# A two-layer hybrid decoder (FoX and NSA attention): narrower last values product, two query projections placed earlier, two more fill steps before the compression's products

## The chip, the cores and the metric

The kernel runs on one core of one Trainium2 chip. The metric is the device time of one execution in microseconds (us), as the median of several runs. The profile is that of one more execution; its span goes from the first to the last instruction that the profiler saw.

Names: PE is TensorE's matmul, PEld its weight load, DVE is VectorE, ACT is ScalarE, POOL is GpSimd, SP is SyncE, which issues most DMAs here.

## The reference

A batch of one, 512 tokens, model width 1024, two layers, float32. Each layer:

```
h    = rmsnorm(x);  proj = h @ w_in
y_a  = fox_attention(q_a, k_a, v_a, log_sigmoid(f_a + b)) @ w_o_fox        # 8 heads of 64, causal
kc,vc = compress(kc), compress(vc)     # blocks of 32 keys, stride 16: gelu(flat @ w1 + b1) @ w2 + b2
o_n  = g0 * attn(q_b, kc, vc) + g1 * attn(q_b, ks, vs, selected) + g2 * attn(q_b, kw, vw, window)
y_b  = o_n @ w_o_nsa                                                       # 8 query heads, 2 key heads
x    = x + (sigmoid(gate_a) * y_a + sigmoid(gate_b) * y_b) @ w_out
x    = x + relu(rmsnorm(x) @ w_up)**2 @ w_down                             # width 4096
```

At the end there is a last rmsnorm. With 512 tokens there are 8 selection blocks and up to 16 may be chosen, and the window is 512 wide, so the selected and the window branch are both plain causal attention.

## The kernel before

**Products in float32r halves.** Every large product is split into a high and a low half: the weight into `wh`, `wl`, the activation into `uh`, `ul` (or `oh`, `ol`). A k-tile is then three matmuls of 512 tokens: `wh` by `uh` (L208), `wh` by `ul` (L209), `wl` by `uh` (L210), in `gemm` (L202). A projection with eight k-tiles is 24 matmuls into one PSUM bank of the tag `mm`; its generator yields after every second k-tile, six matmuls. An output `half` (FoX or NSA output projection) has four k-tiles, 12 matmuls. PSUM has four tags of two banks each: `mm` (projections and outputs), `S` (scores), `PT` (transposed probabilities), `O` (attention output, and the compression's first products).

**Weights.** They arrive by SP's DMA in the order that `order` lists (L166), are rounded to `wh` by ACT (L182) and subtracted into `wl` by DVE (L183). Two `raw`, two `wh` and two `wl` buffers alternate. `order` must list the weights in the order in which the products take them.

**Attention.** A head and branch is a unit: 8 units for FoX, 16 for NSA (selected and window for each head) in each layer. `attend` (L464) runs three units staggered: `scores` of one, `transposes` of the one before, `values` of the one before that. Scores go by four query blocks of 128, each two matmuls (L388, L391) as wide as the causal keys (256, 256, 384, 512), a maximum with mask on DVE (L394), an exponent on ACT (L395); after the fourth block come the reciprocal (L399), NSA's gate (L401) and the scaling of the four blocks (L404). Transposes (L417) put 10 blocks of 128 by 128 in three groups into `PT`; ACT copies each group into `pth` (L426), DVE subtracts into `ptl` (L427). Values (L443) multiply them with the values of four key blocks, 512, 384, 256 and 256 wide, once for `pth` and once for `ptl`. The fourth key block needs only the last 128 queries. Its product reads 256 columns, of which the first 128 are a zero block: the third group is laid out as [zeros, (3,3), (2,2), (3,2)], and two memsets on DVE (L424, L425) write the zeros for each unit. The scores of block 0 are computed 256 wide where 128 are used.

**The fill.** Between the steps of attention, `attend` draws steps from a generator `fill`, 1.8 for each attention step in FoX and 0.95 in NSA. In FoX, `fill1` gives the projections of the next heads and the compression of `kc` and `vc`: 16 copies and some small ones from `tmp` into `ca` on DVE (L502, L504, L507), in two steps, and then the first products (L521, plain float32, `ca` as weights), which alternate with the rest of the projections. In NSA, `fill2` gives the softmax over compressed keys (`cmp_gen`, L578 to L620), the gate projections with their `tanh` (L838, L839), the FoX output `half(0, m)` with its multiplication by the gate into `MA` (L848), and the query projections 2 and 3 (`qproj`), whose rotary part takes two `tmp` buffers (L323 to L327) and whose two halves are copied by SP's DMA into `q` (L362). The tag `tmp` has three buffers, which the gate tiles use too.

A tile scheduler fixes the order of each engine's instructions when the kernel is built, so the order in the trace isn't strictly that of the source. Each engine then works off its queue in order.

Of the kernel before, what the change touches and what calls it, by code (L numbers as in the profile page):

```python
# [11 lines left out]
F32 = mybir.dt.float32  # L12
# [128 lines left out]
class Body:  # L141
# [264 lines left out]
    def transposes(self, u):  # L406
        nc = self.nc
        E = u["E"]
        u["pt"] = []
        for g in range(3):  # L410
            ps = self.p("PT")
            if g < 2:
                todo = [(i, g) for i in range(g, NB)]
            else:
                todo = [(3, 3), (2, 2), (3, 2)]
            for j, (i, b) in enumerate(todo):
                nc.tensor.transpose(ps[:, j * 128:(j + 1) * 128], E[i][:, b * 128:(b + 1) * 128], self.ident)  # L417
            n = 128 * len(todo)
            h = self.t("t2", [128, T], F32R, name="pth")
            lo = self.t("t2", [128, T], F32R, name="ptl")  # L420
            o = 0
            if g == 2:
                o = 128
                nc.vector.memset(h[:, :128].bitcast(F32), 0.0)  # L424
                nc.vector.memset(lo[:, :128].bitcast(F32), 0.0)  # L425
            nc.scalar.copy(h[:, o:o + n], ps[:, :n])  # L426
            nc.vector.tensor_sub(lo[:, o:o + n], ps[:, :n], h[:, o:o + n].bitcast(F32))  # L427
            u["pt"].append((h, lo))
            yield

    def values(self, u):
        nc = self.nc
        if u.get("first", True):
            u["O"][0] = self.p("O")
        O = u["O"][0]
        first = u.get("first", True)
        pt = u["pt"]
        last = u.get("last", True)
        todo = [(0, 0, 0, 512), (1, 1, 0, 384), (2, 2, 256, 256), (3, 2, 0, 256)]
        for b, g, o, n in todo:  # L440
            v = u["v"](b)
            for f in range(2):
                nc.tensor.matmul(O[:, T - n:], v, pt[g][f][:, o:o + n],  # L443
                                 start=first and b == 0 and f == 0, stop=last and b == 3 and f == 1)
            yield
        if "after" in u:
            u["after"]()
# [233 lines left out]
    def order(self, l):  # L681

        a = self.a
        flat = lambda ap: ap.rearrange("p k c -> p (k c)")
        wb = [flat(a["wb"][l, i]) for i in range(32)]
        for c in range(4):
            s = a["wva"][l, c]
            if l == 0 and c == 0:
                yield from ((s[:, j], 512) for j in range(2))
            else:  # L690
                yield flat(s), 1024
        yield from ((flat(a["wg2"][l, c]), 576) for c in range(4))
        for i in (0, 1, 2, 3, 8, 9, 4, 5, 6, 7, 10, 12, 13, 11):
            yield wb[i], 1024
        wo = [[flat(a["wo"][l, f, m]) for m in range(4)] for f in range(2)]
        for m in range(8):
            yield wb[16 + m], 1024
            if m % 2 == 1:
                yield wo[0][m // 2], 1024
            if m in (1, 3):  # L700
                yield wb[14 + m // 2], 1024
        yield from ((wb[24 + m], 1024) for m in range(8))
        yield from ((wo[1][m], 1024) for m in range(4))
        yield from ((flat(a["wout"][l, m]), 1024) for m in range(8))
        for c in range(4):
            yield from ((flat(a["wup"][l, 8 * c + j]), 1024) for j in range(8))
            yield from ((flat(a["wdn"][l, c, m]), 1024) for m in range(8))

    def layer(self, l, u):
        nc, a = self.nc, self.a  # L710
        wb = a["wb"][l].rearrange("m p k c -> m p (k c)")
# [5 lines left out]
        g = self.token_proj(src, 512, va, u)  # L717
# [6 lines left out]
        g = self.token_proj([[a["wg2"][l, c].rearrange("p j m -> p (j m)")] for c in range(4)], 288, g2, u)  # L724
# [35 lines left out]
        def proj(i, key, fn, tag="mm"):  # L760
            def done(ps):
                st[key] = fn(ps)
            return self.block(wb[i], u, done, tag)
# [17 lines left out]
        def fox_proj(p, tags=("mm", "mm")):  # L781
            yield from proj(2 * p, ("ka", p), lambda ps: self.k_pair(self.scaled(ps), p), tags[0])
            yield from proj(2 * p + 1, ("qa", p), lambda ps: self.q_pair(self.scaled(ps), True), tags[1])

        def qproj(p):
            return proj(12 + p, ("qb", p), lambda ps: self.q_pair(self.roped(ps)))

        def cmp_gen(hk):
            yield from self.cmp_probs(hk, [st.get(("qb", p)) for p in range(4)])

        def fill1():
            yield from fox_proj(1)
            yield from proj(8, "kc", self.scaled)
            yield from proj(9, "vc", self.scaled)
            c = self.compress(st["kc"], st["vc"], small, l)
            rest = chain(fox_proj(2), fox_proj(3), proj(10, "ks", lambda ps: self.k_pair(self.roped(ps))),
                         qproj(0), qproj(1))
            yield from alternate(c, rest)
            yield from proj(11, "kw", lambda ps: self.k_pair(self.roped(ps)))

        self.pc = {}
        run(fox_proj(0, ("PT", "PT")))
        self.attend([fox_unit(h) for h in range(8)], fill1(), self.FOX_FILL)


# [23 lines left out]
        def half(kind, m, w):  # L829

            xs = ya if kind == 0 else yb
            ps = self.p("mm")
            yield from self.gemm(ps, w, 4 * (m % 2), xs, ks=4)
            st["y"] = ps

        def gate_tanh(ps, tag="tmp"):
            s = self.t(tag, [128, T], name="gate")
            nc.vector.tensor_mul(s, ps, R)  # L838
            nc.scalar.activation(s, s, AF.Tanh, scale=0.5)  # L839
            return s  # L840

        def gated(m0):
            for m in (m0, m0 + 1):
                yield from proj(16 + m, ("ga", m), gate_tanh)
            w = self.weights(a["wo"][l, 0, m0 // 2].rearrange("p i c -> p (i c)"))
            for m in (m0, m0 + 1):
                yield from half(0, m, w)
                nc.vector.scalar_tensor_tensor(MA[m // 2][:, m % 2], st["ga", m], 1.0, st["y"],  # L848
                                               op0=OP.add, op1=OP.mult)

        def fill2():
            yield from cmp_gen(0)
            yield from gated(0)
            yield from qproj(2)
            yield from gated(2)
            yield from qproj(3)
            yield from cmp_gen(1)
            yield from gated(4)
            yield from gated(6)
            for m in range(8):  # L860
                yield from proj(24 + m, ("gb", m), lambda ps: gate_tanh(ps, ("oh", "ol")[m % 2]))

        units = []
        for h in range(0, 8, 2):
            (a0, b0), (a1, b1) = nsa_units(h), nsa_units(h + 1)
            units += [a0, a1, b0, b1]
        self.attend(units, fill2(), self.NSA_FILL)
        yb = [st["ob", p] for p in range(4)]

# [28 lines left out]
        for m in range(8):  # L898
            ps = self.bank()
# [20 lines left out]
        for c in range(4):  # L920
            acts = []
            for j in range(8):
                ps = self.bank()
# [11 lines left out]
            if c < 3 or l + 1 < L:  # L935
# [3 lines left out]
                for m in range(8):  # L939
                    ps = self.bank()  # L940
# [117 lines left out]
def chain(*gens):  # L1058
    for g in gens:
        yield from g  # L1060


def alternate(a, b):

    live = [a, b]
    while live:
        for g in list(live):
            try:
                next(g)
            except StopIteration:  # L1070
                live.remove(g)
            else:
                yield
# [18 lines left out]
```

## Time and profile before

| | |
|---|---|
| median of 3 runs | 1567.62 us (1567.20 to 1568.24) |
| the profiled execution | 1568.84 us, span 1567.1 us |
| granted TensorE clock, mean | 0.997 |
| busy, share of the span | PE 99%, PEld 82%, DVE 57%, ACT 40%, POOL 17% |
| matmul records | 7580 |

A matmul's duration in the trace is from its start to its modelled end, and matmuls are pipelined: the next one starts before the one ahead has ended. What a product costs in a stream is read from start to start. "[0.70 <-DVE ptl L427]" behind a row is the idle time before it and what ended that.

### The profile page before, as it was taken

The numbers are of one execution on the slowest core, as the hardware profiler recorded it, in microseconds if no ns is written. First come the engines' busy times: TensorE is split into PE (matmuls) and PEld (weight loads), VectorE is DVE, ScalarE is ACT, GpSimd is POOL, SyncE is SP. The second block draws the span as 40 slices with busy tenths as digits, with TensorE's granted clock in tenths as the row PEclk, the third lists the DMA queues.
The fourth block names the chain that finished last, engine by engine and source line by source line (L and its number), as shares of the span: only waits on it lengthen the run. The fifth ranks groups of instructions, "written<-read, shape, count | busy, mean of one in ns | idle before, by whom it ended". The sixth has DMA issues, their size and how long they took to land.

```text
span 1567.1 us, 20162 instructions
## 1 busy us (share of the span) xinstructions
PE 1548.7 (99%) x7580; PEld 1280.8 (82%) x7580; DVE 890.0 (57%) x1815; ACT 631.2 (40%) x1145; POOL 260.0 (17%) x210
## 2 busy tenths in 40 slices
PE   9999999999999999999999999999999999999997
PEld 8877788888888888888887687888888888888887
DVE  5687988866443333333646789887564433333343
ACT  6444655643432222223433456555434312222243
POOL 4000000000241322305400000000002504132252
PEclk9999999999999999999999999999999999999998
DMA  6645522133332233223535543222322322332231
GB/s 234 173 130 148 139 69 82 55 100 105 104 94 95 94 97 104 95 94 101 173 118 164 161 124 105 69 67 65 123 96 94 95 94 94 98 104 94 95 121 54
DMA packets 56624, 169.40 MB, mean 108 GB/s; under 512 B 7344, under 2 KB 8112, under 8 KB 56528
## 3 DMA queue, kind: packets, MB, share of 16 engines
q1 hardware_dynamic: 53072, 161.84, 33.3%
q10 hardware_dynamic: 3456, 6.29, 1.2%
q8 instruction: 59, 0.97, 0.3%
q14 instruction: 37, 0.30, 0.1%
HBM read 140.77 MB, written 4.19 MB: 93 GB/s over the span
## 4 chain that ended last, share of the span: by engine, by line
PE 74%; issue 13%; POOL 6%; DVE 4%; ACT 1%; DMA 1%; SPq 0%; POOLq 0%; DVEq 0%; ACTq 0%
PE ps_mm L208 11%; PE ps_mm L209 11%; PE ps_mm L210 11%; PE ps_O L443 4%; PE ps_PT L417 3%; POOL tmp L916 3%; POOL ol L917 3%; PE ps_S L208 3%; PE ps_S L209 3%; PE ps_S L210 3%; PE ps_PT L208 3%; PE ps_PT L209 3%; PE ps_PT L210 3%; PE ps_O L209 3%; PE ps_O L208 2%
## 5 line engine op out<-in xcount | busy, mean ns | idle before, releaser
L182 ACT CAST wh<-raw 128x1024 fp32r<-128x1024 f32 (+2 forms) x235 | 243.1, 1035 | 619.7 <-PE ps_mm L209 159.6
L183 DVE TENSOR_TENSOR wl<-raw,wh 128x1024 fp32r<-128x1024 f32 (+2 forms) x235 | 287.1, 1222 | 53.2 <-ACT wh L182 44.5
L208 PE MATMUL ps_mm<-uh,wh 128*128 128x512 f32 x608 | 242.1, 398 | 0.0
L210 PE MATMUL ps_mm<-uh,wl 128*128 128x512 f32 x608 | 239.7, 394 | 0.0
L209 PE MATMUL ps_mm<-ul,wh 128*128 128x512 f32 x608 | 239.3, 394 | 0.0
L916 POOL TENSOR_TENSOR tmp<-tmp 128x512 f32<-128x512 f32 x64 | 97.5, 1523 | 439.3 <-ACT oh L915 439.3
L395 ACT ACTIVATE E<-E,mx 128x128 f32<-128x128 f32 x192 | 107.8, 562 | 77.4 <-DVE mx L394 73.3
L208 PEld LDWEIGHTS ps_mm<-uh,wh 128*128 128x128 f32 x608 | 114.3, 188 | 27.0 <-issue 6.9
L210 PEld LDWEIGHTS ps_mm<-uh,wl 128*128 128x128 f32 x608 | 114.3, 188 | 24.1 <-issue 0.8
L209 PEld LDWEIGHTS ps_mm<-ul,wh 128*128 128x128 f32 x608 | 114.7, 189 | 18.8
L208 PE MATMUL ps_mm<-oh,wh 128*128 128x512 f32 (+1 forms) x288 | 111.8, 388 | 3.2 <-DVE gate L838 3.0
L209 PE MATMUL ps_mm<-ol,wh 128*128 128x512 f32 (+1 forms) x288 | 111.8, 388 | 0.7 <-POOL ol L917 0.7
L210 PE MATMUL ps_mm<-oh,wl 128*128 128x512 f32 (+1 forms) x288 | 111.1, 386 | 0.0
L426 ACT CAST pth<-ps_PT 128x512 fp32r<-128x512 f32 x144 | 72.6, 510 | 92.0 <-PE ps_PT L417 91.6
L249 POOL TENSOR_TENSOR acc<-sq 128x512 f32<-128x512 f32 (+1 forms) x6 | 8.4, 1398 | 592.5 <-DVE wl L183 579.8
L394 DVE CUSTOM_DVE_ANT_0 E<-ps_S,ct 128x128 f32<-128x128 f32 x192 | 91.6, 482 | 24.9 <-PE ps_S L391 23.9
L427 DVE TENSOR_TENSOR ptl<-ps_PT,pth 128x512 fp32r<-128x512 f32 x144 | 84.9, 594 | 26.3 <-ACT pth L426 25.7
L417 PE MATMUL ps_PT<-ct,E 128*128 128x128 f32 x480 | 84.9, 275 | 1.9 <-DVE ptl L427 1.4
L917 POOL TENSOR_TENSOR ol<-tmp,oh 128x512 fp32r<-128x512 f32 x64 | 84.7, 1323 | 5.0
L417 PEld LDWEIGHTS ps_PT<-ct,E 128*128 128x128 f32 x480 | 60.2, 140 | 16.8 <-DVE ptl L427 4.5
L208 PEld LDWEIGHTS ps_mm<-oh,wh 128*128 128x128 f32 x288 | 54.2, 188 | 14.4 <-DVE gate L838 4.7
L388 PE MATMUL ps_S<-kd,q 128*128 128x256 f32 x192 | 63.9, 338 | 0.0
(325 smaller groups left out, 3220.8 us busy)
## 6 DMA issues: line engine op xcount, KB each, us to landing
raw<-wb SPq DMA_DIRECT2D x64, 512.0 KB, 3.6
raw<-wup SPq DMA_DIRECT2D x64, 512.0 KB, 4.1
raw<-wdn SPq DMA_DIRECT2D x64, 512.0 KB, 3.5
kd<-hl SPq DMA_DIRECT2D x48, 256.0 KB, 4.9
w<-w SPq DMA_DIRECT2D x32, 256.0 KB, 5.8
q<-hl SPq DMA_DIRECT2D x64, 128.0 KB, 2.8
raw<-wo SPq DMA_DIRECT2D x16, 512.0 KB, 3.5
raw<-wout SPq DMA_DIRECT2D x16, 512.0 KB, 3.6
```

What stands on the lines that cost most here:

```text
L182: nc.scalar.copy(h[:, :n], raw[:, :n])
L183: nc.vector.tensor_tensor(lo[:, :n], raw[:, :n], h[:, :n].bitcast(F32), op=OP.subtract)
L208: mm(ps, h[:, c], xh, start=start and i == 0, stop=False)
L209: mm(ps, h[:, c], xl, start=False, stop=False)
L210: mm(ps, lo[:, c], xh, start=False, stop=stop and i == ks - 1)
L394: nc.vector.tensor_tensor_reduce(e, ps[:, :n], self.mask[:, T - n:], -1.0, BIG, OP.add, OP.min, mx)
L395: nc.scalar.activation(e, e, AF.Exp, bias=mx, scale=-1.0, accum_out=sm[:, i:i + 1])
L417: nc.tensor.transpose(ps[:, j * 128:(j + 1) * 128], E[i][:, b * 128:(b + 1) * 128], self.ident)
L426: nc.scalar.copy(h[:, o:o + n], ps[:, :n])
L427: nc.vector.tensor_sub(lo[:, o:o + n], ps[:, :n], h[:, o:o + n].bitcast(F32))
L916: nc.gpsimd.tensor_tensor(t, t, t, op=OP.mult)
L917: nc.gpsimd.tensor_tensor(lo, t, h.bitcast(F32), op=OP.subtract)
```

## The change

It has three parts.

1. The zero block goes. The third group is laid out as [(3,3), (2,2), (3,2)], without the two memsets, and the fourth key block's two value products are 128 columns wide in place of 256. There are 48 units in the two layers, so 96 memsets go and 96 products become narrower.
2. In NSA's fill, the query projections 2 and 3 come ahead of the FoX outputs of the gate pairs 0 and 2. `gated` is cut into `gates` (two gate projections) and `gated` (two outputs); the order is cmp_gen(0), gates(0), qproj(2), gated(0), gates(2), qproj(3), gated(2), cmp_gen(1), and the rest as before. In `order` the weights of the two query projections change places with those of the FoX outputs.
3. In FoX's fill, the first steps of the compression and of the other projections are drawn by hand: copies, one step of the rest, copies, three steps of the rest. Then the two alternate as before. Before, the alternation gave one step of the rest after the second set of copies ahead of the first products; now there are three.

```diff
@@ transposes
-            o = 0
-            if g == 2:
-                o = 128
-                nc.vector.memset(h[:, :128].bitcast(F32), 0.0)
-                nc.vector.memset(lo[:, :128].bitcast(F32), 0.0)
-            nc.scalar.copy(h[:, o:o + n], ps[:, :n])
-            nc.vector.tensor_sub(lo[:, o:o + n], ps[:, :n], h[:, o:o + n].bitcast(F32))
+            nc.scalar.copy(h[:, :n], ps[:, :n])
+            nc.vector.tensor_sub(lo[:, :n], ps[:, :n], h[:, :n].bitcast(F32))
@@ values
-        todo = [(0, 0, 0, 512), (1, 1, 0, 384), (2, 2, 256, 256), (3, 2, 0, 256)]
+        todo = [(0, 0, 0, 512), (1, 1, 0, 384), (2, 2, 128, 256), (3, 2, 0, 128)]
@@ order
             yield wb[16 + m], 1024
+            if m in (1, 3):
+                yield wb[14 + m // 2], 1024
             if m % 2 == 1:
                 yield wo[0][m // 2], 1024
-            if m in (1, 3):
-                yield wb[14 + m // 2], 1024
@@ fill1
+            for g in (c, rest, c, rest, rest, rest):
+                next(g)
+                yield
             yield from alternate(c, rest)
@@ layer
-        def gated(m0):
+        def gates(m0):
             for m in (m0, m0 + 1):
                 yield from proj(16 + m, ("ga", m), gate_tanh)
+
+        def gated(m0):
             w = self.weights(a["wo"][l, 0, m0 // 2].rearrange("p i c -> p (i c)"))
@@ fill2
             yield from cmp_gen(0)
+            yield from gates(0)
+            yield from qproj(2)
             yield from gated(0)
-            yield from qproj(2)
+            yield from gates(2)
+            yield from qproj(3)
             yield from gated(2)
-            yield from qproj(3)
             yield from cmp_gen(1)
-            yield from gated(4)
-            yield from gated(6)
+            for m in (4, 6):
+                yield from gates(m)
+                yield from gated(m)
```

Behind the memsets' lines the line numbers of the changed kernel are lower by five (L417 stays, L427 becomes L422, L443 becomes L438, L507 becomes L502, L521 becomes L516), and L838 becomes L836.

## The prediction

> **What bounds the kernel now.** I read the page's first part, then the table by stretches of time around the edited places, then TensorE's waits, then the timeline at each of them. TensorE (PE) is busy nearly all the time, and the profiled execution took 1568.84 us, 1.7 us more than its span and 1.2 us more than the median of the three runs (1567.62). So PE's work comes off the time one for one, and otherwise only PE's own stops can be won.
>
> ```profile
> span 1567.1 us, 20162 instructions
> PE 1548.7 (99%) x7580; PEld 1280.8 (82%) x7580; DVE 890.0 (57%) x1815; ACT 631.2 (40%) x1145; POOL 260.0 (17%) x210
> ```
>
> The stretches show where PE stops. Columns: stretch and length, PE, PEld, DVE, ACT, POOL busy, granted clock, DMA share.
>
> ```profile
> 84.00:92.00 8.00, 6.60 (x37) 4.69 (x36) 7.62 (x25) 1.93 (x5) 0.00 (x0) 1.00 0.46 125
> 92.00:176.00 84.00, 84.00 (x434) 63.08 (x433) 67.74 (x177) 42.76 (x96) 2.09 (x4) 1.00 0.54 148
> 184.00:192.00 8.00, 6.50 (x35) 5.21 (x34) 7.94 (x25) 5.43 (x15) 0.00 (x0) 1.00 0.00 0
> 192.00:260.00 68.00, 67.77 (x355) 56.43 (x354) 56.69 (x156) 36.73 (x86) 0.00 (x0) 1.00 0.26 79
> ```
>
> PE loses 1.4 us in the compression (84 to 92 us) and 1.5 us where FoX attention hands over to NSA (184 to 192 us). In both, VectorE (DVE) is full: 7.62 and 7.94 of 8.00 us. In between PE never stops. PE's waits name the same two places (us in total, times, longest), each once per layer:
>
> ```profile
> PE ps_mm L208 <- DVE gate L838: 3.0, 2, 1.5
> PE ps_O L521 <- DVE ca L507: 1.4, 2, 0.7
> PE ps_PT L417 <- DVE ptl L427: 1.4, 2, 0.7
> ```
>
> That is 5.8 us for two layers. Counted from start to start the stops are a little longer. The timeline (start, duration, engine, line) of layer 1's compression:
>
> ```profile
> 87.40 0.65 PE L521 MATMUL ps_O<-w,ca 128*64 128x256 f32 x2
> 88.00 0.68 DVE L427 TENSOR_TENSOR ptl<-ps_PT,pth 128x512 fp32r<-128x512 f32 x1
> 88.69 1.49 DVE L507 COPY ca<-tmp 64x248 f32<-64x248 f32 x4
> 88.74 0.55 PE L417 MATMUL ps_PT<-ct,E 128*128 128x128 f32 x3 [0.70 <-DVE ptl L427]
> 89.05 0.48 PE L391 MATMUL ps_S<-kd,qx 128*128 128x256 f32 x2
> 90.23 0.65 PE L521 MATMUL ps_O<-w,ca 128*64 128x256 f32 x2 [0.70 <-DVE ca L507]
> 90.69 0.27 DVE L394 CUSTOM_DVE_ANT_0 E<-ps_S,ct 128x128 f32<-128x128 f32 x1
> ```
>
> A product's duration overlaps the next one's by about 0.17 us (a 512-wide one shows 0.39 and is followed after 0.23, below). From the first L521 to L417 pass 1.34 us, of which L521 takes 0.65 - 0.17; the stop is 0.86. From L391 to the second L521 pass 1.18 us, of which L391 takes 0.48 - 0.17; the stop is 0.87. Together **1.7 us a layer**. Both are DVE's doing: it works off the copies `ca` (L507) with a split (L427) in their midst. The last row matters below: the maximum of score block 0 (L394) stands behind nearly all the copies too.
>
> The seam, layer 1:
>
> ```profile
> 182.41 0.69 DVE L394 CUSTOM_DVE_ANT_0 E<-ps_S,ct 128x512 f32<-128x512 f32 x1
> 183.28 0.73 ACT L395 ACTIVATE E<-E,mx 128x512 f32<-128x512 f32 x1
> 184.23 0.68 DVE L599 TENSOR_REDUCE s<-tmp 128x16 f32<-128x512 f32 x1
> 184.83 0.17 DVE L399 RECIPROCAL rr<-sm 128x4 f32<-128x4 f32 x1
> 186.91 0.39 PE L210 MATMUL ps_mm<-uh,wl 128*128 128x512 f32 x1
> 188.05 0.69 DVE L838 TENSOR_TENSOR gate<-ps_mm,R 128x512 f32<-128x512 f32 x1
> 188.65 0.69 DVE L607 TENSOR_TENSOR tmp<-tmp,s 128x512 f32<-128x512 f32 x1
> 188.79 0.50 PE L208 MATMUL ps_mm<-oh,wh 128*128 128x512 f32 x1 [1.50 <-DVE gate L838]
> ...
> 189.13 0.39 PE L209 MATMUL ps_mm<-ol,wh 128*128 128x512 f32 x1
> 189.36 0.40 PE L210 MATMUL ps_mm<-oh,wl 128*128 128x512 f32 x1
> ```
>
> The first product of the FoX output (188.79, `oh`) needs a free `mm` bank; both hold gate projections, and DVE reads the first only at 188.05, behind the softmax of the compressed scores. A 512-wide product takes 0.23 us (189.13 to 189.36), so of the 1.88 us since 186.91 **1.65 us a layer** is a stop. If every stop at both places went, both layers would win 2 x (1.7 + 1.65) = 6.7 us. That is the most that moving steps can bring.
>
> **Part 1, the narrower product.** 48 units (8 FoX and 16 NSA in each layer) lose two memsets and get two 128-wide products in place of 256-wide ones.
>
> ```profile
> L424 DVE MEMSET pth<- 128x128 f32 x48 | 7.9, 165 | 0.0
> L425 DVE MEMSET ptl<- 128x128 f32 x48 | 7.9, 165 | 0.0
> 196.90 0.28 PE L443 MATMUL ps_O<-ptl,vn 128*128 128x256 f32 x1
> 197.01 0.28 PE L443 MATMUL ps_O<-pth,vn 128*128 128x256 f32 x1
> 197.13 0.28 PE L443 MATMUL ps_O<-ptl,vn 128*128 128x256 f32 x1
> 53.82 0.83 PE L664 MATMUL ps_S<-ones,f 128*8 128x128 f32 x6
> 54.48 0.38 PE L665 MATMUL ps_S<-ct,f 128*8 128x128 f32 x2
> 204.47 0.57 PE L417 MATMUL ps_PT<-ct,E 128*128 128x128 f32 x3
> 204.80 0.48 PE L210 MATMUL ps_mm<-uh,wl 128*128 128x512 f32 x1
> ```
>
> The memsets' 15.8 us of DVE lie beside PE's work; they count only where DVE is full, and there (one unit, two memsets) they give up to 0.33 us a place. A 256-wide value product goes every 0.115 us (197.13 less 196.90, halved). No product of this type under 256 wide is in the trace, so the price of 128 is open. Nearest rows: the transposes, 128 wide with a 128-column weight load each and one record each, go every 0.11 us (204.47 to 204.80, three of them); the plain float32 products of L664, 128 wide and two records a product, take 0.11 us a record (54.48 less 53.82, by six), 0.22 a product. The changed program issues the narrow product as one instruction, like the transposes, so I take 0.11 us: the weight load sets the pace and 96 products win 96 x 0.006 = **0.6 us**. The high end is the float32 pace, 96 x (0.22 - 0.115) = 10.1 us lost. The low end is a pure column count: a quarter of a 512-wide product's 0.23 us, 0.057, which wins 96 x 0.058 = 5.6 us. [...]
>
> **Part 2, three steps ahead of the compression's products.** Fill steps move, their work stays. In the changed order two more steps of projections, 12 products or 2.7 us, stand ahead of the first L521, and the second stop with `ca` goes: the copies are done by then. But the queue of PE also carries the next unit's scores. Its 384-wide block (L388) now stands ahead of the transposes and of L521, and its `S` bank is freed by the maximum of block 0. On DVE that maximum stays behind the same 13 copies; only the two memsets are gone from in front of it. By the row at 90.69 it ends at 90.96, in the changed kernel some 0.3 earlier, about 90.65. PE gets to the block after what stood ahead of 87.40 in the trace, six more projection products and two 256-wide score products: 87.40 + 6 x 0.23 + 2 x 0.12 = 89.0. So it stops there for about 1.6 us in place of 1.7. I book **0.1 us won a layer**, with 1.7 (it clears) and -0.5 (it waits for `S` and then again behind it) as ends.
>
> **Part 3, the query projections ahead of the FoX output.** No work is added. The next product after the two gate projections is now one of query projection 2, on `uh`; it needs the same `mm` bank, freed by the same DVE read of gate 0. The operands were never what PE waited for. On DVE the order shifts: ahead of the gate stand the 512-wide maximum, a reciprocal that waits for ScalarE's exponent (182.41 to 184.83 above shows this round: 2.4 us), then the steps of the softmax and of a head's output, 0.6 us for a 512-wide one by 184.23 to 184.83. From the score product that starts the round (0.45 before its maximum) I get 0.45, 1.7 to 2.4 to the reciprocal, six 512-wide steps at 0.6, four scalings and three small steps, 1.9 together: the gate is read after 7.7 to 8.3 us, and the maximum that frees an `S` bank, two steps of 0.6 sooner, after 6.5 to 7.1. PE's path from the same product holds 5.7 us of work to the score block that needs the bank (18 products of 512, 4.1 us, seven of 256 or less, two of 384 and four transposes, 1.6 us), and 0.45 more to the projection. It stops 0.8 to 1.4 us for the bank and some 0.75 us for the gate: 1.6 to 2.1 against 1.65. I book **0.2 us lost a layer**, ends -1.65 and +2.
>
> Later, the outputs `half(0,0)` and `half(0,1)` follow each other with nothing between them but attention; each of two pairs can wait for the product with the gate that empties the bank. I book 0.1 us a pair, 0.2 a layer, up to 1.4 if two 0.69 us steps of DVE are waited for in full. The DMAs move too: projection 2's weights are fetched ahead of the first FoX output weights, and the `q` copies (L362) go ahead of the second. SP, which issues them, waits for buffers and not for data:
>
> ```profile
> SPq L166 <- DVE wl L183: 1019.1, 190, 18.7
> ```
> ```profile
> raw<-wb SPq DMA_DIRECT2D x64, 512.0 KB, 3.6
> ```
>
> A weight fetch held behind `q` has two gate projections and a query projection (72 products, 16 us) before its use. I book nothing; without that cover it would be a 512 KB load's 3.6 us. What NSA loses otherwise is small (0.23 us in the 68 us after the seam, in the table by stretches) and may move by 0.5 us a layer.
>
> **The sum.** 2 x (-0.1 + 0.2 + 0.2) - 0.6 = 0.0 us: 1568.8 for a profiled run, **1567.6** at the median's level. 0.2% of the time, 3.1 us, is about what a measurement can tell from no change. With the bounds of parts 2 and 3 this case runs from 1563.5 to 1571.5.
>
> **Rivals.**
> *Both stops go* (chance 0.20, 1560.3): DVE, relieved of memsets, reaches the maximum and the gate before PE does. For it: 12 more products at one place, and at the other 24 on operands that are long there. Against: DVE is full in both stretches and none of its steps there goes but two memsets. Price 6.7 + 0.6 us.
> *The narrow product falls to the float32 pace* (0.24, 1578.3): one mechanism, in all 48 units: 10.1 us lost where 0.6 were booked as won. It decides as soon as a 128-wide product takes over 0.15 us (96 x 0.035 = 3.4 us). For it: no product of this type under 256 wide is in the trace, block 0's scores are 256 wide where 128 columns are used, and a float32 product of that width costs 0.22 us. Against: the single instruction.
> *The buffers bind at the seam* (0.10, 1572.8): two gate tiles lie in two of the three `tmp` buffers while the rotary of the query projection needs two, so its second waits until the first output is multiplied with its gate; two DVE steps of 0.69 us stand in PE's way at two places in each layer, 4 x 1.4 = 5.6 us in place of the 0.4 booked. It decides where too few attention products lie between.
> *The column count sets the narrow product's pace* (0.06, 1562.6): the low end above, 5.6 us won in place of 0.6.
> *The forecast* (0.40).
>
> Faster by over 0.2%: 0.20 + 0.06 and 0.03 of the forecast's own spread, 0.29. Slower: 0.24 + 0.10 and 0.04, 0.38. Within: 0.33. The range goes from just above the first rival to just above the second, 1561 to 1579.
>
> **What would show it.** In the changed profile: the narrow products' spacing (0.11, 0.06 or 0.22 us); a wait of the 384-wide L388 for L394 in the compression in place of those for `ptl` and `ca`; at the seam a wait of L208 on `uh` for the gate, with one for an `S` bank before it; PE's busy time nearly unchanged. I am wrong if the two stretches show PE full, or if a narrow product takes over 0.15 us.

## The result and the profile after

| | before | changed |
|---|---|---|
| median of 5 runs | 1567.68 us (1567.20 to 1568.24) | 1574.50 us (1572.66 to 1576.82) |
| ratio, 95% interval | | 1.0045 (1.0031 to 1.0060) |
| profiled execution, span | 1567.1 us | 1570.6 us |
| granted clock, mean, by run | 0.997 | 0.996, 0.996, 0.995, 0.995, 0.994 |

The change makes the kernel 6.8 us slower. Its five runs spread over 4 us where the five of the kernel before spread over 1, but 27 more runs of the kernel before, made beside the first experiments, spread over 4 as well (1566.37 to 1570.46), at a clock of 0.997 to 0.998. The profiled execution of the changed kernel is the fastest of its five, so its trace shows only part of the loss. One of the 11 runs of `e1_narrow`, the profiled one, took 3123 us (span 3121.4 us, granted clock 1.000) and is left out below.

The page after, its first part, and PE's waits (us in total, times, longest):

```profile
span 1570.6 us, 20073 instructions
PE 1550.2 (99%) x7580; PEld 1281.6 (82%) x7580; DVE 878.4 (56%) x1719; ACT 632.6 (40%) x1145; POOL 260.2 (17%) x210
```
```profile
PE ps_S L388 <- DVE mx L394: 6.5, 4, 2.0
PE ps_S L388 <- issue: 1.7, 2, 1.0
...
PE ps_mm L208 <- DVE gate L836: 0.9, 2, 0.5
...
PE ps_mm L208 <- DVE tmp L325: 0.4, 2, 0.2
PE ps_mm L208 <- DVE ma L848: 0.3, 2, 0.2
PE ps_PT L417 <- DVE ptl L422: 0.2, 1, 0.2
```

The two waits of the compression (for `ptl` and `ca`) are gone, as they should be, and so is most of the gate's at the seam, where FoX attention hands over to NSA. In their place stands one name, the `S` bank that the score maximum frees: four stops, 6.5 us, where the old three rows held 5.8. Two further stops of about 1 us have no releaser named ("issue"). The same stretches of time as before:

```profile
84.00:92.00 8.00, 6.00 (x32) 4.90 (x31) 7.66 (x26) 1.59 (x5) 0.00 (x0) 0.97 0.38 104
92.00:176.00 84.00, 82.74 (x414) 60.24 (x414) 60.78 (x152) 40.23 (x94) 2.09 (x4) 0.98 0.51 142
184.00:192.00 8.00, 6.41 (x33) 4.84 (x31) 6.89 (x21) 5.03 (x11) 0.00 (x0) 1.00 0.60 158
192.00:260.00 68.00, 67.68 (x356) 56.21 (x357) 58.49 (x156) 39.54 (x92) 0.00 (x0) 1.00 0.26 78
90.10:95.10 5.00, 4.97 (x19) 3.15 (x20) 4.47 (x11) 3.71 (x9) 0.00 (x0) 0.66 0.02 4
```

PE now loses 2.0 us in the compression where it lost 1.4, and 1.3 us between 92 and 176 us, where it lost nothing. And the clock column moves: 0.97, 0.98, and 0.66 over the five microseconds behind the stop. PE's timeline at that place, layer 1:

```profile
87.74 0.39 PE L210 MATMUL ps_mm<-uh,wl 128*128 128x512 f32 x1
90.13 0.45 PE L388 MATMUL ps_S<-kd,q 128*128 128x384 f32 x1 [2.00 <-DVE mx L394]
...
91.15 0.39 PE L208 MATMUL ps_mm<-uh,wh 128*128 128x512 f32 x1
91.38 0.50 PE L209 MATMUL ps_mm<-ul,wh 128*128 128x512 f32 x1
91.68 0.63 PE L210 MATMUL ps_mm<-uh,wl 128*128 128x512 f32 x1
92.11 0.63 PE L208 MATMUL ps_mm<-uh,wh 128*128 128x512 f32 x1
92.53 0.63 PE L209 MATMUL ps_mm<-ul,wh 128*128 128x512 f32 x1
```

From 87.74 to 90.13 are 2.39 us, 2.16 more than a product takes. Below this is called the joined stop: one in the compression where there were two. A good microsecond later the products go every 0.43 us (92.11 to 92.53) in place of 0.23: TensorE runs at half its clock (0.50 granted between 91.60 and 94.90). By 0.66 over 5.0 us that lasts 2 x 0.34 x 5.0 = 3.4 us and costs half of it, 1.7 us. In layer 2 the same stop (2.38 us at 864.07) isn't followed by such a fall in this execution.

The two stops put down to "issue" stand at the end of FoX attention. Layer 1's, all engines:

```profile
172.10 0.28 PE L438 MATMUL ps_O<-ptl,vf 128*128 128x128 f32 x1
172.29 0.67 DVE L394 CUSTOM_DVE_ANT_0 E<-ps_S,ct 128x512 f32<-128x512 f32 x1
172.90 0.07 DVE L394 DVE_READ_ACCUMULATOR2_ANT mx<- 128x1 f32 x1
172.90 0.67 DVE L327 TENSOR_TENSOR tmp<-tmp 128x512 f32<-128x512 f32 x1
...
173.34 0.36 PE L388 MATMUL ps_S<-kd,q 128*128 128x256 f32 x1 [0.96 <-issue]
```

The score product at 173.34 is the first of the NSA unit and reads a NSA query `q`. No row names what it waits for, but the DMA packets in the trace show it: the last packet of that query's four copies ends at 173.45, and in layer 2 at 947.68, where the product starts at 947.62. That is the far end of what part 3 did, and the experiments follow it back.

### The profile page after: what moved, and what is told of

It reads as the page before. It is cut to its first block, busy times and chain, and to the rows that moved or that the text cites. A ratio compares the mean times of both kernels' runs of the same rounds, so it can differ in the third digit from the quotient of the medians.

```text
span 1570.6 us, 20073 instructions
## 1 busy us (share of the span) xinstructions
PE 1550.2 (99%) x7580; PEld 1281.6 (82%) x7580; DVE 878.4 (56%) x1719; ACT 632.6 (40%) x1145; POOL 260.2 (17%) x210
## 4 chain that ended last, share of the span: by engine, by line
PE 90%; DVE 7%; ACT 1%; issue 1%; DMA 0%; DVEq 0%; SPq 0%; ACTq 0%
PE ps_mm L208 12%; PE ps_mm L209 12%; PE ps_mm L210 12%; PE ps_S L208 4%; PE ps_S L210 4%; PE ps_S L209 4%; PE ps_PT L208 4%; PE ps_PT L209 4%; PE ps_PT L210 4%; PE ps_O L210 4%; PE ps_O L209 4%; PE ps_O L208 4%; PE ps_O L438 3%; PE ps_PT L417 3%; PE ps_S L388 2%; PE ps_S L391 2%
## 5 line engine op out<-in xcount | busy, mean ns | idle before, releaser
L210 PE MATMUL ps_mm<-uh,wl 128*128 128x512 f32 x608 | 239.3, 394 | 0.0
L210 PEld LDWEIGHTS ps_mm<-uh,wl 128*128 128x128 f32 x608 | 114.4, 188 | 23.3
L210 PE MATMUL ps_mm<-oh,wl 128*128 128x512 f32 (+1 forms) x288 | 110.8, 385 | 0.0
L422 DVE TENSOR_TENSOR ptl<-ps_PT,pth 128x512 fp32r<-128x512 f32 x144 | 85.1, 597 | 26.9 <-ACT pth L421 26.3
L417 PE MATMUL ps_PT<-ct,E 128*128 128x128 f32 x480 | 84.0, 276 | 0.5 <-DVE ptl L422 0.2
L417 PEld LDWEIGHTS ps_PT<-ct,E 128*128 128x128 f32 x480 | 59.7, 141 | 14.6 <-issue 2.4
```

Source lines behind the costliest of these rows:

```text
L210: mm(ps, lo[:, c], xh, start=False, stop=stop and i == ks - 1)
L422: nc.vector.tensor_sub(lo[:, :n], ps[:, :n], h[:, :n].bitcast(F32))
```

## The experiments

The theory behind the experiments (A): the loss is made of PE's stops: the joined one in the compression with the clock's fall behind it, and those of the late NSA queries. Rivals: the narrow products (B), the projections' new place (C).

**The three parts apart.** Each kernel is one of the two with parts of the diff taken back.

`e1_narrow`, part 1 on the kernel before. 

> The kernel before with part 1 alone (no zero block, 128-wide last values product). Theory A (the loss is made of stops of PE: one joined stop of 2.2 us in each layer's compression, after which the TensorE clock may fall to half for some 3.4 us; a longer seam; a new 1 us stop at the last FoX unit): the narrow products go every 0.108 us, so 0.6 to 1 us is won, about 1567 us, clock 0.997, spread of the runs under 1 us, and the compression keeps its two separate stops of 0.9 us. Rival B (the 96 narrow products or the layout without zeros make the loss): 1573 to 1575. If the new 1 us stop at the last FoX unit (1.1 and 0.9 us in the changed kernel) comes from this part: about 1569.

Measured: 1566.81 us as the median of the ten runs that are kept (1563.66 to 1569.47), ratio 0.9995 (0.9986 to 1.0004). B falls.

`e2_order`, part 2 on the kernel before. 

> The kernel before with part 2 alone (query projections 2 and 3 ahead of the FoX outputs). Theory A: the seam stops for 2.0 us in place of 1.66 and two short waits of 0.2 to 0.4 us come with the gated outputs, so 1 to 2 us are lost: 1568.6 to 1569.6, clock 0.997, small spread. Rival C (this part makes the whole loss): 1572 to 1575.

Measured: 1564.76 us, ratio 0.9979 (0.9970 to 0.9988): 3.0 us faster. A had this part as a loss; both A's figure and C fall.

`e3_steps`, part 3 on the kernel before. 

> The kernel before with part 3 alone (two more fill steps ahead of the compression's products). Theory A: the two stops of 0.87 us join in one of about 2.2 us in each layer; 0.8 us is lost by that, and 1.7 to 2.2 us more for each layer in which the clock falls to half behind it: 1568.4 without, 1570 to 1573 with, runs spread over 2 us or more, mean clock 0.994 to 0.996. Rival C (part 2 makes the loss): 1567.6, small spread, clock 0.997.

Measured: 1578.01 us (1577.27 to 1581.81), ratio 1.0071 (1.0058 to 1.0084), mean clock 0.993 to 0.996. Part 3 is the whole loss, and more than A had for it. Its waits, from the profiled run, which was the slowest of the five (the first row is the joined stop):

```profile
PE ps_S L388 <- DVE mx L394: 4.6, 2, 2.3
PE ps_mm L208 <- DVE gate L841: 3.6, 2, 1.8
PE ps_mm L208 <- DVE tmp L325: 3.1, 2, 1.6
PE ps_S L388 <- DVE tmp L327: 2.1, 1, 2.1
...
PE ps_S L388 <- DMA q<-hl: 0.4, 1, 0.4
```

L325 and L327 are steps of the rotary of the NSA key and query projections, which holds the `mm` bank that PE wants (L325) and makes the `q` that the first NSA scores need. The stop that is put down to L327 ends at 174.66; that L327 belongs to a later projection and is over at 173.67, while the last packet of the query's copies ends at 174.67. So here too it is the copies.

`e4_no_steps`, the changed kernel with part 3 taken back. 

> The changed kernel without part 3 (parts 1 and 2). Theory A: two separate stops in the compression, no fall of the clock, 1568 to 1570 us with a spread under 1 us; the time that part 3 adds on top of it is 4 to 6 us. Rival C: 1573 to 1575, as the changed kernel.

```diff
-            for g in (c, rest, c, rest, rest, rest):
-                next(g)
-                yield
             yield from alternate(c, rest)
```

Measured: 1565.39 us, ratio 0.9985 (0.9976 to 0.9994): 9.1 us better than the changed kernel, where A had 4 to 6. So without part 3 the change would have won 2.3 us. The gate's wait at the seam is no longer among its waits, and the compression's two stops have joined without part 3 too:

```profile
PE ps_O L516 <- DVE ca L502: 3.7, 2, 1.9
```

Here the clock falls as well. A stretch of layer 2 behind the stop:

```profile
860.00:866.00 6.00, 6.00 (x24) 4.10 (x25) 3.78 (x15) 2.17 (x7) 0.00 (x0) 0.72 0.10 40
```

`g1_one_three`, parts 1 and 3, and `g2_narrow`, part 1 once more for a trace. 

> Parts 1 and 3 without part 2. Theory A (part 3's loss doesn't need part 2, and part 2 wins its 2 to 3 us in NSA's small stops whatever else is done): 1576 to 1578. Rival C (part 2 has a share in the loss): 1570 to 1573.

> Part 1 alone once more, for a trace of it. Theory A: the order in the compression is that of parts 1 and 2, one joined stop of 2.0 us in each layer in place of two of 0.86, with a fall of the clock behind some of them; the seam keeps its 1.7 us if part 2 is needed to remove it, or shows 0.4 us if part 1 does it alone. Time 1566.5 to 1567.5.

Measured: 1577.28 us, ratio 1.0062 (1.0049 to 1.0076), and 1566.76 us, ratio 0.9994 (0.9985 to 1.0003). Part 3 costs 10.3 us alone, 10.5 on part 1, 9.1 on parts 1 and 2: it needs neither. In g2_narrow's trace PE stops 0.43 us at the seam (193.27) and 2.04 us in the compression, in each layer: part 1 alone takes most of the one away and joins the other. How it does so was not followed.

**What part 3 does: the rotary behind the tail.** The last step of the compression ends in a tail of small steps on DVE (L527 to L570 after, five lines later before), which takes the three `tmp` buffers in turn. The rotary of the NSA key projection, the next to ask for `tmp`, stands behind it. DVE before:

```profile
147.10 0.23 DVE L560 STREAM_SHUFFLE tmp<-tmp 128x64 f32<-128x64 f32 x1
...
148.05 0.73 DVE L323 STREAM_SHUFFLE tmp<-ps_mm 128x512 f32<-128x512 f32 x1
...
151.74 0.69 DVE L327 TENSOR_TENSOR tmp<-tmp 128x512 f32<-128x512 f32 x1
...
156.38 0.68 DVE L327 TENSOR_TENSOR tmp<-tmp 128x512 f32<-128x512 f32 x1
```

and after:

```profile
151.41 0.22 DVE L555 STREAM_SHUFFLE tmp<-tmp 128x64 f32<-128x64 f32 x1
...
154.05 0.75 DVE L323 STREAM_SHUFFLE tmp<-ps_mm 128x512 f32<-128x512 f32 x1
...
156.50 0.68 DVE L327 TENSOR_TENSOR tmp<-tmp 128x512 f32<-128x512 f32 x1
```

The tail comes 4.3 us later (147.10 to 151.41) since the compression's products start later. The first rotary starts 6.0 us later (148.05 to 154.05) and comes to its last step 4.8 us later (151.74 to 156.50), though its projection was no later. The last of that projection's 24 products, before and after:

```profile
141.26 0.39 PE L210 MATMUL ps_mm<-uh,wl 128*128 128x512 f32 x1
140.71 0.39 PE L210 MATMUL ps_mm<-uh,wl 128*128 128x512 f32 x1
```

`e9_tail` takes the tail off `tmp`:

```diff
-        g = self.t("tmp", [128, 4, 64], name="g")
+        g = self.t("t2", [128, 4, 64], name="g")
...
-        v = self.t("tmp", [128, 2, 64])
+        v = self.t("t2", [128, 2, 64], name="tv")
```

> The changed kernel with the small tiles of the compression's tail in the tag t2 in place of tmp. Theory A (part 3 makes the compression's tail some 4 us later, and the rotary of the NSA key and query projections queues behind the tail for the three tmp buffers, so the first NSA scores wait for their q): the rotary goes ahead of the tail, the stops of 1.1 and 0.9 us at the last FoX unit go, 2 to 4 us are won against 1574.5: 1570.5 to 1572.5; the stop of 2.2 us in the compression stays. Rival F (the last unit's stop comes from the DMA alone or from the longer attention): 1574 to 1575.

Measured: 1569.07 us (1568.18 to 1572.03), ratio 1.0010 (1.0001 to 1.0018): 5.4 us won against the changed kernel, more than expected. The first rotary is now done ahead of the tail's last steps, with its own last one at 145.77:

```profile
145.77 0.68 DVE L327 TENSOR_TENSOR tmp<-tmp 128x512 f32<-128x512 f32 x1
...
151.58 0.23 DVE L555 STREAM_SHUFFLE tsh<-tk 128x64 f32<-128x64 f32 x1
```

The first NSA query's copies follow. SP's row for them before, after and in e9_tail:

```profile
163.21 2.39 SPq L362 DMA_DIRECT2D q<-hl  x4
167.22 2.75 SPq L362 DMA_DIRECT2D q<-hl  x4
159.71 2.39 SPq L362 DMA_DIRECT2D q<-hl  x4
```

Both stops at the last FoX unit are gone, and the seam's two stops (1.40 and 0.64 us in each layer of the changed kernel) are down to one of 0.63. The joined stop is still there (2.17 us).

**The joined stop: DVE's copies.** `e6_act` is the changed kernel, `e7_act` parts 1 and 2, each with half of the copies on ACT:

```diff
-                        nc.vector.tensor_copy(t[half][r * 64:(r + 1) * 64, :, h, :31],
-                                              v[h * 64:(h + 1) * 64, r, :, half:half + 31])
+                        (nc.vector.tensor_copy if x is kc else nc.scalar.copy)(
+                            t[half][r * 64:(r + 1) * 64, :, h, :31],
+                            v[h * 64:(h + 1) * 64, r, :, half:half + 31])
```

> The changed kernel with the eight copies of the second compression input issued on ACT in place of DVE. Theory A: the joined stop of 2.2 us in each layer and the clock's fall behind it go, 4 to 7 us won: 1567.5 to 1570.5. The stops at the last FoX unit (1.1, 0.9) and at the seam (2.0 each) stay. Rival E: less than 2 us won.

> Parts 1 and 2 without part 3, with the eight copies of the second compression input issued on ACT in place of DVE. Theory A (DVE's copies are what PE stops for): the stop of 2.03 us in each layer goes almost wholly, and with it the fall of the clock: 4 us and 1 to 1.7 us won against 1565.39, 1560 to 1561.5. Rival E (ACT's casts of the transposed probabilities queue behind its copies and PE stops for those): 1564 to 1567.

Measured: 1570.67 us, 3.8 better than the changed kernel, a little under the expected 4; and 1559.63 us (1559.39 to 1560.32), ratio 0.9948 (0.9934 to 0.9961), 5.8 better than parts 1 and 2. In e7_act the joined stop is 0.75 us and the runs spread over 1 us. DVE's queue was what PE stopped for.

`f1_both` puts both mendings into the changed kernel. 

> The changed kernel with both mendings: eight compression copies on ACT, and the tail's small tiles in t2. Theory A (the two are separate costs of part 3): 3.8 + 5.4 us add up, 1565.3, about the level of parts 1 and 2 without part 3 (1565.4). If they are one cost: 1568 to 1569.

Measured: 1563.52 us, ratio 0.9971 (0.9961 to 0.9982): 11.0 us won where the two alone add up to 9.2. They are separate costs. The 1.8 us on top are about what one fall of the clock costs: the traces of e6_act and e9_tail still show one fall each, that of f1_both none. That this is the reason was not tried.

**The clock's fall by itself.** `e8_busy` has parts 1 and 2 with eight useless products where PE would stop:

```diff
...
         hp = self.p("O")
+        for i in range(8):
+            nc.tensor.matmul(hp, busy[0][:, :128], busy[0], start=True, stop=True)
         for c in range(8):
...
```

> Parts 1 and 2 without part 3, with eight useless 512-wide products (their result is overwritten) put into PE's queue where it stops for 2.03 us in the compression: 8 x 0.227 = 1.8 us of work in the place of idle time. Theory A (a joined stop of 2 us lets the TensorE clock fall to half for some 3.4 us, sometimes): the stop shrinks to about 0.2 us, the clock no longer falls behind it, and 1 to 1.7 us are won against the same kernel without them (1565.39): 1563.7 to 1564.5, mean clock 0.998. Rival D (the clock's falls cost nothing that matters): 1565.4 or a little more.

Measured: 1563.39 us (1562.92 to 1564.31), ratio 0.9971 (0.9960 to 0.9983), mean clock 0.997 to 0.998 in every run where e4_no_steps had 0.995 to 0.997. The timeline shows the eight (L508) in the place of the stop:

```profile
86.25 0.62 PE L508 MATMUL ps_O<-uh 128*128 128x512 f32 x2
86.71 0.40 PE L391 MATMUL ps_S<-kd,qx 128*128 128x256 f32 x2
86.94 1.55 PE L508 MATMUL ps_O<-uh 128*128 128x512 f32 x6
88.42 0.65 PE L518 MATMUL ps_O<-w,ca 128*64 128x256 f32 x2
89.31 0.65 PE L518 MATMUL ps_O<-w,ca 128*64 128x256 f32 x2 [0.24 <-DVE ca L502]
```

3.6 us of useless work in two layers, and the kernel is 2.0 us faster. The order wins nothing there: PE starts again at 89.31 here and at 90.11 in e4_no_steps, but the same product ahead of the place (the first L210 behind 84 us) already stands at 85.32 and 86.16, 0.84 us apart, for a slower start of that execution. The clock is worth about the whole win: as a mean over the runs it rose from 0.9959 to 0.9973, and 0.0014 x 1563 = 2.2 us (an estimate, as each run's clock is on record to 0.001). `f4_busy` tries the same in the changed kernel. 

> The changed kernel with eight useless 512-wide products (overwritten) in PE's queue ahead of the score block at which it stops for 2.2 us in the compression. Theory A: the stop shrinks to 0.4 us, PE's end of the stretch stays, and only the clock's falls behind it go, 1 to 2 falls of about 2 us each: 1571 to 1573, mean clock 0.997, smaller spread. Rival D (the clock's falls don't matter, or come from elsewhere): 1574 to 1576.

Measured: 1574.27 us (1572.31 to 1575.00), ratio 1.0039 (1.0027 to 1.0052): a miss. The stop shrank to 0.4 us as expected, no half clock follows it in the trace, and the mean clock rose to 0.996 to 0.998 in the five runs, but the time stayed and the runs still spread over 2.7 us. The mean over the runs rose from 0.9952 to 0.9968, by the same estimate 2.5 us, so about as much was lost elsewhere, and the changed kernel's spread isn't the clock's alone. The stops at the last FoX unit differ from layer to layer (1.33 and 0.45 us in this trace) and hang on copies; that they make the rest was not tried.

**Versions that beat both.** `f2_best` is e7_act with the tail on t2, `f3_act12` is e7_act with 12 of the 16 copies on ACT (`x is kc and half == 0`). 

> Parts 1 and 2, eight copies on ACT, and the tail's tiles in t2. Theory A: without part 3 the rotary doesn't queue long behind the tail, so nothing is left for t2 to win: 1559.6, within 1 us. If the tmp queue costs something here too: 1557 to 1558.

> Parts 1 and 2, with 12 of the 16 compression copies on ACT. Theory A: the last stop of 0.75 us a layer in the compression goes: 1558 to 1559. Rival E (ACT's casts queue behind the copies): 1560 to 1562.

Measured: 1561.47 us, ratio 0.9959 (0.9946 to 0.9971), worse than without t2 by 1.8; and 1559.04 us (1558.52 to 1560.59), ratio 0.9947 (0.9934 to 0.9959), the lowest of all, though not told apart from e7_act. f1_both and f2_best differ in part 3 alone: with both mendings in, part 3 costs 2.0 us in place of 9.1. The compression stretch of f3_act12 has PE full, and DVE no longer:

```profile
84.00:92.00 8.00, 7.95 (x42) 5.50 (x42) 4.38 (x17) 6.98 (x14) 0.00 (x0) 1.00 0.47 126
```

## Why the prediction was wrong

It forecast no change, 1567.6; the measured 1574.5 lies in its range but on the slower side, and not by one of its rivals as they stood. The parts are called here as in the section on the change; the prediction numbers 2 and 3 the other way round. Its bounds of 1563.5 to 1571.5 don't follow from its own ends: added up, those of the two moves give 1560.7 to 1572.4, and 1574.8 with the 1.4 us of the two pairs.

**Part 3 is the step that failed** (the prediction's "three steps ahead of the compression's products"): 0.1 us won a layer was booked, with 0.5 lost as its end. Part 3 costs 9 to 10.5 us in two layers. Two things were left out, and one row was misread. First, the walk ended at the compression's first products. What was pushed later was the whole chain behind them, to the tail that holds `tmp`, and through that ring the NSA key's and queries' rotary, the `mm` bank, the first NSA scores and the seam: 5.4 us by e9_tail. The prediction had the `tmp` ring as a rival, but at the seam, with the gate tiles as holders, and with a chance of 0.10. Second, the stop was priced by its length alone. One stop of 2 us isn't two of 0.9: the clock can fall behind it. By the mean clocks of the runs, 0.9977 in the 27 of the kernel before and 0.9952 in the changed one, falls make some 3.9 of the 6.8 us (an estimate as above). That cost is not part 3's alone, though: parts 1 and 2 have the joined stop too, and by their 0.9959 lose some 2.8 us to it.

Third, the length itself. The new wait was named rightly, the 384-wide score block for the maximum behind the copies; it came out at 2.16 us where 1.6 were worked out and the old pair made 1.7. The executions have to be set against each other first: the transposes ahead of the place stand at 84.09 us before and at 83.14 after, so the changed one is 0.95 ahead. With that added, PE came at 88.92, as the walk had it (89.0), but the bank was free at 91.02 and not at 90.65. The maximum got no earlier than before (90.97), because the two memsets that the walk takes from in front of it don't stand there. The nearest in this layer of the kernel before are at 77.72 and here:

```profile
93.52 0.17 DVE L424 MEMSET pth<- 128x128 f32 x1
```

**Part 1: the wrong row was taken.** No float32 pace: that rival falls. But the forecast pace of 0.11 us a product is only half true. From the changed kernel:

```profile
167.65 0.28 PE L438 MATMUL ps_O<-ptl,vf 128*128 128x256 f32 x1
167.76 0.22 PE L438 MATMUL ps_O<-pth,vf 128*128 128x128 f32 x1
167.82 0.28 PE L438 MATMUL ps_O<-ptl,vf 128*128 128x128 f32 x1
167.93 0.39 PE L388 MATMUL ps_S<-kd,q 128*128 128x384 f32 x1
```

The first of the pair is followed after 0.06 us (57 to 61 ns in all 48), the second after 0.11 (108 to 113 ns in 39 of them). That is 0.085 in the mean, and 48 x (0.23 - 0.17) = 2.9 us won in place of 0.6. That the weight load sets the pace, from which the 0.6 us came, no run shows: each of the two has a load of 128 columns of its own (384 loads for the 384 products of L438), and the second starts 0.06 us behind the first all the same. The transposes, which the prediction preferred, were the wrong neighbour. Part 1 alone still moves the time only by 0.9 and 1.1 us (e1_narrow, g2_narrow), inside its intervals: g2_narrow's trace has the joined stop, and a fall of the clock behind one of the two, against that. The time goes with the clock: the three runs of e1_narrow with a mean clock of 0.998 took 1563.66 to 1565.04 us, the three with 0.995 took 1568.26 to 1569.47.

**Part 2** was booked as 0.4 us lost a layer; it wins 3.0 us alone. At the seam the changed kernel shows what was worked out, a stop of 1.40 us for an `S` bank and one of 0.64 for the gate, 2.0 together where 1.6 to 2.1 were forecast. That is luck: g1_one_three, without part 2, has the same pair, and e2_order, with part 2 alone, has one stop of 1.7 us for the gate as before. The gain lies in NSA attention, which was given 0.5 us a layer either way: from the first score product of its second unit to the last one of all pass 154.7 us before and 153.1 in e2_order, in layer 2 154.4 and 153.0. Which of its small stops go was not followed further.

**Not additive.** Parts 1 and 2 win about 1.0 and 3.0 alone and 2.3 together. The joined stop comes with part 1 and with part 3, not with part 2; by the mean clocks its falls cost some 1.7 us in e1_narrow, none in e2_order and 2.8 in e4_no_steps, which is the larger part of the difference.

## What to carry to other kernels

When steps are moved ahead of a consumer, follow the consumer's own chain to its end, and ask which shared buffers its last step holds and who is next in that ring; here the stop showed up two stages later under another name. Take a stop away at the queue that the engine waits for: putting 12 copies on ACT (40% of the span busy) won 6 us where moving steps lost 9. Two stops of 1 us and one of 2 us didn't cost the same on TensorE here: in the two profiled executions no fall of the clock followed the pairs of 0.86 and 0.87, and one followed one of the two joined stops.

## What the runs showed of the hardware

- Behind some of PE's stops TensorE ran at half clock for about 3.4 us (changed kernel: 0.66 granted over 5.0 us, 0.50 over the 3.3 us from 91.60; e4_no_steps: 0.72 over 6.0 us). In the traces of before, of the changed kernel and of the experiments there are 15 stops of 2.0 to 2.4 us, and 8 were followed by it; of 8 pairs of 1.4 and 0.64 us, a score block apart, 2; of 6 stops of 1.7 us that stood alone, none. Why one stop is followed by it and another isn't was not shown.
- A 128-wide float32r product was followed after 0.058 us by another of its pair, a quarter of a 512-wide one's 0.23, and the second was followed after 0.11 us, about as behind a 256-wide one (0.115). The float32 pace of 0.22 us doesn't show.
